# Modulation sums dealt one per weight granule, a vector's end in three steps, and y's parts made from PSUM

## The chip, the core and the metric

The kernel runs on one core of a Trainium2 chip. The metric is the device time of one execution in microseconds (us), lower is better. Of before there are three timed runs and one profiled execution. Engines in the profile: PE is TensorE (matmul), PEld its weight load, DVE is VectorE, ACT ScalarE, POOL GpSimd, SP SyncE, whose queue issues the DMAs.

## The reference

Two layers over 512 latent tokens and 256 context tokens, D = 2048, all fp32. Both begin with a modulated RMS norm whose shift, scale and gate come from a conditioning vector, and end in a gated residual. Cut to what matters here:

```python
def adaln(cond, w, b):
    m = jax.nn.silu(cond) @ w + b          # w is 2048 x 6144, one for each layer
    return jnp.split(m, 3, axis=-1)        # shift, scale, gate

def even_layer(...):
    h = modulate(rms_norm(x, norm_g), sh, sc); hc = the same of ctx
    kc_t, vc_t = split(hc @ w_in[K, V columns])
    au, av, ag, bq, bk, bv, bg = split(h @ w_in)   # each 1024 wide
    q, k = rope(rms_norm per 64 columns of bq, bk)
    o = (softmax(q0 k0) - lam * softmax(q1 k1)) @ v   # 8 heads, 512 x 768
    y = concat(gelu(au) * spatial(gelu(av)) * silu(ag), rms_norm(o) * silu(bg))
    return x + gt * (y @ w_out)

def odd_layer(...):
    h = modulate(rms_norm(x, norm_g), sh, sc)
    a, b, g = split(h @ w_in)              # each 2048 wide
    y = silu(layer_norm(depthwise_conv31(a * sigmoid(b)))) * silu(g)
    return x + gt * (y @ w_out)
```

## The kernel before, in words

**Products in three passes.** Every large product is fp32 made of three matmuls with split operands: high part by high part, high by low, low by high. A weight granule is 1 MB. `load_w` loads it on SP into one of three `raw` buffers (L95), ACT casts it to `whi` (L103), and DVE or POOL subtracts to get `wlo` (L104); `whi` and `wlo` have two buffers each. PE then runs the granule's matmuls (L67).

**The order of the work.** The program is written block after block: the even layer's early modulation (L304), then the blocks K, BV, K (second half), BV, Q (two), AV (two), U (two) of its input product, then the attention, into whose gaps a "fill stream" (`fill_stream`, 18 granules: gates bg and ag, and the first columns of the output product) is dealt, then the output projection (`og` 1 to 3 and a last piece with `x1_last`), then the odd layer: its input product in groups a, b, g with the convolution on DVE (L1106), the layer norm (`ln_chain`), and the last product with `o_w_out`. A scheduler places each instruction in its engine's own queue, by dependencies and priorities; each engine then runs its queue in order. Buffers come from pools that rotate, so a transfer is issued only when the buffer's last reader is done.

**The modulation sums.** Four vectors of 2048 are not needed at once: gt1 (kind 0, the even layer's gate, needed for the output projection), A2 and sh2 (kinds 1 and 2, the odd layer's scale and shift, needed for `x1_last` and `make_h2`) and gt2 (kind 3, needed for the last product). They are made off PE: `ada_jobs` lists 16 steps for each, 64 in all. A step (`ada_step`) loads 1 MB of the modulation weight through the same three `raw` buffers and adds it, scaled by one column of silu(c), to `acc` on DVE (L461 and L463). The sum over the 128 partitions comes at a vector's 16th step: four fp32 matmuls with ones (L468) and a copy on ACT (L472), four matmuls with `sel4` that turn the row into columns (L475) and additions on DVE (L488 to L499), and for three of the kinds a transposition (L482), a copy (L484) and a store to DRAM (L485). Before, all that follows the 16th step at once.

**How they are dealt.** A block calls a hook once for each of its four granules; the hook runs `ada_step` one, two or three times. Before, BV, K, BV take three, two and three, so 32 sums, which are kinds 0 and 1, lie in these blocks; Q and AV take one for each granule (16) and U two (16). All 64 are done by the end of U (the assert ahead of `p12.close()`), and kind 3's end stands there, ahead of the spatial gate's last matmuls (L67, tile z) and the attention.

**Around the attention.** For each of 32 turns PE makes scores S from kk and qq, DVE takes the maximum (mx, L814), ACT the exponential, DVE the weights of the two softmaxes (w, e: L828 to L830), PE transposes (t, L842), ACT and DVE split the transposed values into ph and pl (L112), and at every second turn PE makes oT from ph, pl and vv. Between these stand the fill's matmuls (tile fm).

**The layer norm's chain.** `ln_chain` runs between the granules of the g groups: mean, squares, `rb3`, then for each of 16 tiles `zs` in steps of four, a product with rb3 (L1149), an activation (L1150), a tanh into PSUM (`z4`, L1152) and (th + 1) * z into SBUF (L1153). After the chain comes the product with `sgs` (L1164), and `split` gives y2h (ACT, L111) and y2l (DVE, L112), which are the last product's stationary operands.

Of the kernel before, what the change touches and what calls it, by code (L numbers as in the profile page):

```python
# [19 lines left out]
P = 128  # L20
D = 2048
KT = D // P
# [23 lines left out]
def hybrid_layers_kernel(  # L46
# [403 lines left out]
    ada_state = {"i": 0, "acc": None}  # L450

    def ada_step(zalloc, n=1):
        for _ in range(n):
            if ada_state["i"] >= len(ada_jobs):
                return
            W, c0, kind, jt = ada_jobs[ada_state["i"]]
            ada_state["i"] += 1
            raw = load_raw(W, jt * P, 1, c0, D)[:, 0, :]
            if jt == 0:
                ada_state["acc"] = ap_.tile([P, D], F32, tag="acc", name=nm("acc"))  # L460
                V.tensor_scalar(ada_state["acc"], raw, sc_[:, 0:1], None, op0=ALU.mult)  # L461
            else:
                V.scalar_tensor_tensor(ada_state["acc"], raw, sc_[:, jt : jt + 1], ada_state["acc"], op0=ALU.mult, op1=ALU.add)  # L463
            if jt == KT - 1:
                acc = ada_state["acc"]
                z = zalloc(T)
                for g in range(4):
                    PE.matmul(  # L468
                        z[32 * g : 32 * g + 32, :], ones[:, 0:32], acc[:, g * T : (g + 1) * T],
                        start=True, stop=True, skip_group_check=True,  # L470
                    )
                A.copy(acc[:, 0:T], z)  # L472
                z = zalloc(KT)
                for i in range(4):
                    PE.matmul(z[:, 4 * i : 4 * i + 4], acc[:, i * P : (i + 1) * P], sel4, start=True, stop=True)  # L475
                z = z.rearrange("p (i g) -> p g i", g=4)
                v4 = lambda a: a.rearrange("p (g i) -> p g i", i=4)


                def row_out(col, row_s):  # L480
                    zr = zalloc(P)
                    PE.transpose(zr[:KT, :], col, ident)  # L482
                    rw = cp.tile([KT, P], F32, tag="rw", name=nm("rw"))
                    V.tensor_copy(rw, zr[:KT, :])  # L484
                    SP.dma_start(row_s.rearrange("(k p) -> k p", p=P), rw)  # L485

                if kind == 0:
                    V.tensor_tensor(v4(gt1), z, v4(g1[:, cEB + 2 * KT : cEB + 3 * KT]), op=ALU.add)  # L488
                    row_out(gt1, gt1_s)
                elif kind == 1:  # L490
                    V.tensor_tensor(v4(A2), z, v4(o_b1), op=ALU.add)
                    V.tensor_tensor(A2, A2, g2[:, cOG : cOG + KT], op=ALU.mult)
                    row_out(A2, A2_s)
                elif kind == 2:
                    V.tensor_tensor(v4(sh2), z, v4(g2[:, cOB : cOB + KT]), op=ALU.add)
                else:

                    V.tensor_tensor(v4(gt2), z, v4(g2[:, cOB + 2 * KT : cOB + 3 * KT]), op=ALU.add)
                    V.tensor_scalar(gt2, gt2, 0.25, None, op0=ALU.mult)  # L499
                    row_out(gt2, gt2_s)  # L500


    def qk_post(ps, which, tt, half, tok0, dst, rope):
# [54 lines left out]
        for b in range(NT):  # L558
            qk_post(ps[b], 0, b, half, b * P, q_s, True)

    hook, hook2, hook3 = (lambda gi, n=n: ada_step(zt, n) for n in (1, 2, 3))
    k_done(k0ps, 0)
    ps = m_block(e_w_in, C_BV, both(), psA, "m", hook3)
    v_done(ps, 0)


# [32 lines left out]
        V.tensor_scalar(lam, lam, LAMBDA_INIT, None, op0=ALU.add)  # L599
        V.tensor_scalar(nlam, lam, -1.0, None, op0=ALU.mult)  # L600

    ps = m_block(e_w_in, C_K + 512, both(), psA, "m", hook2)
    k_done(ps, 1)
    ps = m_block(e_w_in, C_BV + 512, both(), psA, "m", hook3)
    v_done(ps, 1)
    for hb in range(2):
        ps = m_block(e_w_in, C_Q + 512 * hb, lat(), psA, "m", hook)
# [43 lines left out]
    for ug in range(2):  # L651
        ps = t_group(e_w_in, C_U + 512 * ug, hm, psA, "m", hook=hook2)
        for j in range(4):
# [14 lines left out]
            mx = bp.tile([P, T], F32, tag="mx", name=nm("mx"))  # L668
            V.tensor_tensor(mx, z, gu, op=ALU.mult)
            SP.dma_start(ug_s[g], mx)  # L670
    assert ada_state["i"] == len(ada_jobs)
    p12.close()


# [38 lines left out]
    def fill_stream():  # L713
        jobs = []
        for i in range(4):
            jobs += [("bg", i, e_w_in, C_BG + 256 * i), ("ag", i, e_w_in, C_AG + 256 * i)]
        jobs.append(("y", 0, e_w_out, 0))
        grans = [(n, gi) for n in range(9) for gi in range(2)]

        def load(n, gi):  # L720
            return load_w(jobs[n][2], gi * 8 * P, 8, jobs[n][3], 2 * P, G)

        nxt = load(0, 0)
        for x, (n, gi) in enumerate(grans):
            kind, i = jobs[n][:2]
            w, nxt = nxt, (load(*grans[x + 1]) if x + 1 < len(grans) else None)
            if gi == 0:
                ps = ps0 if kind == "y" else [None, None]
            if (n, gi) == (7, 1):
                for kt in [0, 1, 2, 3, 4, 5, 8]:  # L730
                    y_load(kt)
            if (n, gi) == (8, 0):
                for kt in range(9, 14):
                    y_load(kt)
            seq = [(j, k) for j in range(2) for k in range(8)]
            if kind == "y" and gi == 1:
                seq = [(j, k) for j in range(2) for k in range(6)] + [(j, k) for k in (6, 7) for j in range(2)]
            for j, k in seq:
                kt = 8 * gi + k
                if ps[j] is None:  # L740
                    ps[j] = psM.tile([P, T], F32, tag="m", name=nm("fm"))
                if kind == "y":
                    if kt == KT - 1 and j == 0:
                        yield "last"
                    yh, yl = ym[kt]
                    wh, wl = w[0][:, k, :], w[1][:, k, :]

                    for i in range(2):
# [12 lines left out]
                if kt == KT - 1:  # L761
                    th = at.tile([P, T], F32, tag="th", bufs=1, name=nm("th"))
                    A.activation(th, ps[j], AF.Tanh, scale=0.5)
                    if kind == "bg":
                        sg = at.tile([P, T], F32, tag="sbg", bufs=2, name=nm("sbg"))
                        V.scalar_tensor_tensor(sg, th, 1.0, ps[j], op0=ALU.add, op1=ALU.mult)
                        sbg[2 * i + j] = sg
                    else:
                        V.scalar_tensor_tensor(th, th, 1.0, ps[j], op0=ALU.add, op1=ALU.mult)
                        y_out(2 * i + j, th, None)  # L770
                yield "more"
# [260 lines left out]
    for og in range(1, 4):  # L1032
        ps = [mt() for _ in range(NT)]
        for gi in range(KT // 4):
            w = load_w(e_w_out, gi * 512, 4, 512 * og, 512)
            m_granule(ps, ystat, *w, range(4 * gi, 4 * gi + 4), 4 * gi)
            if gi == 0 and og == 1:
                for t in range(NT):
                    x1_done(t, 0, 256, ps0[t // 2][:, 256 * (t % 2) : 256 * (t % 2) + 256], 0)
# [5 lines left out]
        for t in range(NT):  # L1045
            x1_done(t, 512 * og, T, ps[t], og)
    load_x(4)
    wl_ = [load_w(e_w_out, gi * 1024, 8, 256, 256) for gi in range(2)]
    ps = [mt() for _ in range(NT)]
    part = lambda t, gi: m_granule([ps[t][:, 0:256]], [ystat[t]], *wl_[gi], range(8 * gi, 8 * gi + 8), 8 * gi)  # L1050
    for t in range(2):
        for gi in range(2):
            part(t, gi)
        x1_last(t, ps[t][:, 0:256])
        if t == 0:
            for u in range(NT):
                scale(u, 3, T)
# [3 lines left out]
    for t in range(2, NT):  # L1061
        part(t, 1)
        x1_last(t, ps[t][:, 0:256])
    make_h2(0, (8, 16))
    a01 = [mt(), mt()]
    first = t_half_steps(o_w_in, 0, h2, a01, G, None, HALVES)
    next(first)
# [64 lines left out]
    def ln_chain():  # L1132
# [14 lines left out]
        rb3 = token_rstd(vacc, 0, T, 1.0 / D)  # L1147
        for i in range(KT):
            V.tensor_tensor(zs[i], zs[i], rb3, op=ALU.mult)  # L1149
            A.activation(zs[i], zs[i], AF.Identity, bias=g2[:, cLB + i : cLB + i + 1], scale=g2[:, cLG + i : cLG + i + 1])  # L1150
            th = z4()
            A.activation(th, zs[i], AF.Tanh, scale=0.5)  # L1152
            V.scalar_tensor_tensor(zs[i], th, 1.0, zs[i], op0=ALU.add, op1=ALU.mult)  # L1153
            if i % 4 == 3:
                yield

    chain = ln_chain()
    for gi in range(1, 4):
        g_group(gi, lambda gi: next(chain, None))
    for _ in chain:  # L1160
        pass
    y2m = []
    for i in range(KT):
        V.tensor_tensor(zs[i], zs[i], sgs[i], op=ALU.mult)  # L1164
        hi, lo = htile("y2h"), htile("y2l")
        split(hi, lo, zs[i])
        y2m.append((hi, lo))


    gt2b = row_tiles(gt2_s, "gt2b")  # L1170
# [56 lines left out]
```

## Time and profile before

| | us |
|---|---|
| median of 3 runs | 1881.65 |
| lowest and highest | 1880.64, 1884.06 |
| the profiled execution | 1877.36 |
| its span | 1875.6 |
| PE busy | 1816.8 |
| DVE busy | 1135.5 |
| ACT busy | 560.2 |
| POOL busy | 452.8 |

The span is the time from the first to the last instruction that the profile shows; 1.8 us of the execution lie outside it. Windows and rows give times from the span's start. A row of the timeline has start, duration, engine, line, operation, tiles (out<-in), the shape, the count, and in brackets the idle time before it with what ended it. PE's matmuls are pipelined, so their durations overlap. The granted clock (PEclk) is 1.00 at full speed.

### The profile page before, as it was taken

To read this page: it belongs to the slowest core of one execution; us is meant where nothing else is said; L and a number is where in the kernel's file an instruction comes from. 1 tells how busy PE (TensorE), PEld (TensorE's weight loads), DVE (VectorE), ACT (ScalarE), POOL (GpSimd) and SP (SyncE) were. 2 spreads that over 40 slices of the span, in tenths; PEclk is the share of its full clock that TensorE was granted. 3 is DMA by queue.
4 is the path that set the end of the run, shared out by engine and by line. 5 is a ranking of instruction groups with operands and counts; after the bars stand their busy time and mean duration, and the time that the engine had idled before them with its cause. 6 is when DMAs were issued, how large, how long until landed. Compare 5 with 4: busy or idle time off the path is not lost.

```text
span 1875.6 us, 21933 instructions
## 1 busy us (share of the span) xinstructions
PE 1816.8 (97%) x8767; PEld 1484.1 (79%) x8767; DVE 1135.5 (61%) x1571; ACT 560.2 (30%) x747; POOL 452.8 (24%) x173
## 2 busy tenths in 40 slices
PE   5998999999999999999999999999999999999998
PEld 2556877788888878888888889888888888887887
DVE  4339528647746626676664345239999999775111
ACT  3322111122233215444442224322222222463110
POOL 0003002001100022232320002234544544444432
PEclk9999999999999989999999999999999999999999
DMA  9998757776756866576555443232233233223441
GB/s 310 334 330 292 233 177 276 262 249 220 243 186 238 308 164 166 151 194 171 167 193 178 147 135 124 68 108 95 90 102 101 90 95 108 90 90 139 138 160 56
DMA packets 208487, 327.34 MB, mean 175 GB/s; under 512 B 10249, under 2 KB 116610, under 8 KB 200194
## 3 DMA queue, kind: packets, MB, share of 16 engines
q1 hardware_dynamic: 208386, 325.94, 53.9%
q8 instruction: 69, 1.13, 0.2%
q14 instruction: 32, 0.26, 0.0%
HBM read 292.33 MB, written 33.58 MB: 174 GB/s over the span
## 4 chain that ended last, share of the span: by engine, by line
PE 85%; DMA 6%; DVE 4%; issue 2%; ACT 1%; POOL 1%; SPq 0%; DVEq 0%; POOLq 0%; ACTq 0%
PE tg L67 30%; PE m L67 18%; PE mb L67 16%; PE fm L67 10%; DMA raw<-in_e_ada_w_dram 2%; PE S L67 2%; DVE acc L463 2%; PE oT L67 2%; DMA raw<-in_o_ada_w_dram 2%; PE z L304 2%; PE t L842 1%; DVE wlo L104 1%; PE z L67 1%; DMA x<-in_x_dram 1%; PE fm L752 1%
## 5 line engine op out<-in xcount | busy, mean ns | idle before, releaser
L104 POOL TENSOR_TENSOR wlo<-raw,whi 128x2048 fp32r<-128x2048 f32 x80 | 370.0, 4624 | 647.0 <-ACT whi L103 639.6
L103 ACT CAST whi<-raw 128x2048 fp32r<-128x2048 f32 x136 | 259.8, 1910 | 740.2 <-PE tg L67 214.1
L1106 DVE SCALAR_TENSOR_TENSOR z<-y,dwc,z 128x512 f32<-128x512 f32 x480 | 319.2, 744 | 0.1
L67 PE MATMUL tg<-h2h,wlo 128*128 128x512 f32 x704 | 274.7, 390 | 0.0
L67 PE MATMUL tg<-h2l,whi 128*128 128x512 f32 x704 | 273.9, 389 | 0.0
L67 PE MATMUL tg<-h2h,whi 128*128 128x512 f32 x704 | 270.4, 389 | 0.0
L104 DVE TENSOR_TENSOR wlo<-raw,whi 128x2048 fp32r<-128x2048 f32 x56 | 128.1, 2288 | 146.3 <-ACT whi L103 146.3
L67 PE MATMUL mb<-whi,hhi 128*128 128x512 f32 x512 | 204.8, 403 | 5.3 <-DVE tn L512 3.4
L67 PE MATMUL mb<-wlo,hhi 128*128 128x512 f32 x512 | 203.4, 397 | 2.3 <-DVE wlo L104 2.3
L67 PE MATMUL mb<-whi,hlo 128*128 128x512 f32 x512 | 203.6, 398 | 0.0
L463 DVE SCALAR_TENSOR_TENSOR acc<-raw,silu_c,acc 128x2048 f32<-128x2048 f32 x60 | 140.9, 2349 | 87.2 <-DMA raw<-in_o_ada_w_dram 65.1
L67 PEld LDWEIGHTS tg<-h2h,wlo 128*128 128x128 f32 x704 | 132.1, 188 | 28.0 <-issue 0.5
L67 PEld LDWEIGHTS tg<-h2l,whi 128*128 128x128 f32 x704 | 132.1, 188 | 27.8 <-issue 0.5
L67 PEld LDWEIGHTS tg<-h2h,whi 128*128 128x128 f32 x704 | 132.1, 188 | 27.4
L194 POOL TENSOR_TENSOR rs<-ms,mhalf 128x8 f32<-128x8 f32 x20 | 44.6, 2244 | 394.4 <-DVE ms L193 394.4
L67 PEld LDWEIGHTS mb<-whi,hhi 128*128 128x128 f32 x512 | 98.1, 192 | 39.7 <-issue 14.0
L67 PEld LDWEIGHTS mb<-wlo,hhi 128*128 128x128 f32 x512 | 98.3, 192 | 23.0 <-DVE wlo L104 3.1
L67 PEld LDWEIGHTS mb<-whi,hlo 128*128 128x128 f32 x512 | 98.3, 192 | 20.9
L67 PE MATMUL fm<-hhi,whi 128*128 128x512 f32 x256 | 106.7, 417 | 0.0
L67 PE MATMUL m<-wlo,y2h 128*128 128x512 f32 x256 | 99.8, 390 | 2.6 <-POOL wlo L104 2.6
L67 PE MATMUL fm<-hlo,whi 128*128 128x512 f32 x256 | 101.1, 395 | 0.0
L67 PE MATMUL fm<-hhi,wlo 128*128 128x512 f32 x256 | 100.8, 394 | 0.0
(259 smaller groups left out, 3024.9 us busy)
## 6 DMA issues: line engine op xcount, KB each, us to landing
raw<-in_e_w_in_dram SPq DMA_DIRECT2D x56, 1024.0 KB, 5.2
raw<-in_o_ada_w_dram SPq DMA_DIRECT2D x48, 1024.0 KB, 5.8
raw<-in_o_w_in_dram SPq DMA_DIRECT2D x48, 1024.0 KB, 5.1
raw<-in_e_ada_w_dram SPq DMA_DIRECT2D x64, 512.0 KB, 7.5
raw<-in_e_ada_w_dram SPq DMA_DIRECT2D x16, 1024.0 KB, 5.6
raw<-in_e_w_out_dram SPq DMA_DIRECT2D x16, 1024.0 KB, 5.9
raw<-in_o_w_out_dram SPq DMA_DIRECT2D x16, 1024.0 KB, 5.9
qq<-q_s SPq DMA_DIRECT2D x16, 512.0 KB, 8.7
```

What stands on the lines that cost most here:

```text
L67: return PE.matmul(o, l, r, start=start, stop=stop)
L103: A.copy(hi, raw)
L104: (lo_eng or V).tensor_tensor(lo, raw, hi.bitcast(F32), op=ALU.subtract)
L194: G.tensor_tensor(dst, tmp, mhalf[:, 0:1].broadcast_to([P, n]), op=ALU.pow)
L304: PE.matmul(ada_ps[j][32 * g : 32 * g + 32, 0 : 2 * nc_], S[:, kt, :], raw[:, i, :], start=(kt < 4), stop=(kt >= KT - 4), skip_group_check ...
L463: V.scalar_tensor_tensor(ada_state["acc"], raw, sc_[:, jt : jt + 1], ada_state["acc"], op0=ALU.mult, op1=ALU.add)
L752: PE.matmul(o_, a[:, ts_], b, start=(kt == 0 and i == 0 and a is yh and b is wh), stop=(kt == KT - 1 and i == 1 and a is yl), skip_group_c ...
L842: PE.transpose(z[:, k * P : (k + 1) * P], e[:, (k0 + k) * P : (k0 + k + 1) * P], ident)
L1106: V.scalar_tensor_tensor(zi if t == TAPS - 1 else z, y2[:, t : t + T], w(t), z, op0=ALU.mult, op1=ALU.add)
```

## The change

**The sums.** `hook3` is gone and BV, K, BV take one step for each granule (12). Q and AV keep one and U two, so 44 steps lie ahead of the attention instead of 64. In the fill stream three granules of four take one, and the output projection takes one for each of its 12 granules; the assert moves behind it. **A vector's end.** The 16th step only puts three functions, `spread`, `columns` and `row`, into `ada_tail`; each later call runs one of them, and `spread` alone takes the place of a sum. Kind 3's last steps stand behind `x1_last`. **y's parts.** The products with rb3 are all made first. Where the gate `sgs[i]` is there already, (th + 1) * z and the product with it are written to th in PSUM, and `y2_split` makes the parts from there; the others are made after the chain, through a PSUM tile too.

```diff
     def ada_step(zalloc, n=1):
+        if ada_tail:
+            f = ada_tail.pop(0)
+            f(zalloc)
+            if f.__name__ == "spread":
+                return
         for _ in range(n):
...
             if jt == KT - 1:
-                acc = ada_state["acc"]
-                z = zalloc(T)
...
+                ada_tail.extend(ada_finish(kind, ada_state["acc"]))
+                return
...
+    def ada_finish(kind, acc):
+        col, b_, row_s = bias[kind]()
+
+        def spread(zalloc):
+            z = zalloc(T)
+            for g in range(4):
+                PE.matmul(
+                    z[32 * g : 32 * g + 32, :], ones[:, 0:32], acc[:, g * T : (g + 1) * T],
+                    start=True, stop=True, skip_group_check=True,
+                )
+            A.copy(acc[:, 0:T], z)
+
+        def columns(zalloc):
+            z = zalloc(KT)
+            for i in range(4):
+                PE.matmul(z[:, 4 * i : 4 * i + 4], acc[:, i * P : (i + 1) * P], sel4, start=True, stop=True)
...
+        def row(zalloc):
+            zr = zalloc(P)
+            PE.transpose(zr[:KT, :], col, ident)
...
+            SP.dma_start(row_s.rearrange("(k p) -> k p", p=P), rw)
+
+        return [spread, columns] + ([row] if row_s is not None else [])
...
-    ps = m_block(e_w_in, C_BV, both(), psA, "m", hook3)
+    ps = m_block(e_w_in, C_BV, both(), psA, "m", hook)
...
-    ps = m_block(e_w_in, C_K + 512, both(), psA, "m", hook2)
+    ps = m_block(e_w_in, C_K + 512, both(), psA, "m", hook)
...
-    ps = m_block(e_w_in, C_BV + 512, both(), psA, "m", hook3)
+    ps = m_block(e_w_in, C_BV + 512, both(), psA, "m", hook)
...
-    assert ada_state["i"] == len(ada_jobs)
     p12.close()
...
             if gi == 0:
                 ps = ps0 if kind == "y" else [None, None]
+            if x % 4 != 3:
+                ada_step(zt3, 1)
...
             m_granule(ps, ystat, *w, range(4 * gi, 4 * gi + 4), 4 * gi)
+            ada_step(z4, 1)
...
+    assert ada_state["i"] == len(ada_jobs)
...
         x1_last(t, ps[t][:, 0:256])
+        ada_step(z4)
...
+    while ada_tail:
+        ada_step(z4)
...
         for i in range(KT):
             V.tensor_tensor(zs[i], zs[i], rb3, op=ALU.mult)
+        for i in range(KT):
             A.activation(zs[i], zs[i], AF.Identity, bias=g2[:, cLB + i : cLB + i + 1], scale=g2[:, cLG + i : cLG + i + 1])
             th = z4()
             A.activation(th, zs[i], AF.Tanh, scale=0.5)
-            V.scalar_tensor_tensor(zs[i], th, 1.0, zs[i], op0=ALU.add, op1=ALU.mult)
+            if sgs[i] is None:
+                V.scalar_tensor_tensor(zs[i], th, 1.0, zs[i], op0=ALU.add, op1=ALU.mult)
+            else:
+                V.scalar_tensor_tensor(th, th, 1.0, zs[i], op0=ALU.add, op1=ALU.mult)
+                V.tensor_tensor(th, th, sgs[i], op=ALU.mult)
+                y2_split(i, th)
             if i % 4 == 3:
                 yield
+                if i == 7:
+                    yield
...
-    y2m = []
     for i in range(KT):
-        V.tensor_tensor(zs[i], zs[i], sgs[i], op=ALU.mult)
-        hi, lo = htile("y2h"), htile("y2l")
-        split(hi, lo, zs[i])
-        y2m.append((hi, lo))
+        if y2m[i] is None:
+            z = z4()
+            V.tensor_tensor(z, zs[i], sgs[i], op=ALU.mult)
+            y2_split(i, z)
```

On DVE, at the end of the first K block, whose results tn, rot and ms are k's normalisation and rotation while the BV block's matmuls begin, there stood before:

```order
L463 SCALAR_TENSOR_TENSOR acc_1524<-raw_1610,silu_c,acc_1524 128x2048
L512 TENSOR_TENSOR tn_1301<-mb_330,rs_1297 128x512
L193 TENSOR_SCALAR ms_1346<-ms_1346 128x8
L193 TENSOR_SCALAR ms_1371<-ms_1371 128x8
L508 TENSOR_REDUCE ms_1396<-sq_1394 128x8
L512 TENSOR_TENSOR tn_1326<-mb_331,rs_1322 128x512
L463 SCALAR_TENSOR_TENSOR acc_1524<-raw_1613,silu_c,acc_1524 128x2048
L104 TENSOR_TENSOR wlo_1535<-raw_1532,whi_1534 128x2048
L520 TENSOR_TENSOR rot_1303<-tn_1301,SG_1291 128x16x16 x2
```

Now the same tiles come so:

```order
L522 TENSOR_TENSOR tn_1301<-mb_330,rs_1297 128x512
L193 TENSOR_SCALAR ms_1371<-ms_1371 128x8
L468 SCALAR_TENSOR_TENSOR acc_1524<-raw_1685,silu_c,acc_1524 128x2048
L530 TENSOR_TENSOR rot_1303<-tn_1301,SG_1291 128x16x16 x2
L522 TENSOR_TENSOR tn_1326<-mb_331,rs_1322 128x512
L518 TENSOR_REDUCE ms_1396<-sq_1394 128x8
L104 TENSOR_TENSOR wlo_1529<-raw_1526,whi_1528 128x2048
```

One sum stands among these posts where there were two, and the posts follow each other more closely behind it. On PE, at the end of U (tiles tg) and ahead of the spatial gate (z_4594 and on), there stood before:

```order
L67 MATMUL tg_4333<-hlo_1185,whi_4516 128x512
L468 MATMUL z_4574<-acc_4069,ones 32x512 x4
L475 MATMUL z_4580<-sel_84,acc_4069 128x4 x4
L482 MATMUL z_4587<-ident,gt_98 16x128
L67 MATMUL z_4594<-wsh,vnh_3981 128x128
L67 MATMUL z_4594<-wsl,vnh_3981 128x128
```

Now U's last matmuls are followed by the gate's second tile and the fill's first (fm):

```order
L67 MATMUL tg_4235<-hlo_1185,whi_4431 128x512
L67 MATMUL z_4510<-wsl,vnh_3908 128x128
L67 MATMUL z_4510<-wsh,vnl_3912 128x128
L67 MATMUL z_4529<-wsh,vnh_3887 128x128
...
L67 MATMUL z_4548<-wsh,vnl_3912 128x128
L67 MATMUL fm_4605<-hhi_390,whi_4592 128x512
```

The end of kind 3 is gone from this place, and the gate's first tile and most of its second stand earlier, among U's own matmuls. On DVE in the attention, at the end of the sixth turn, there stood before, between the next turn's maximum (mx) and its weights (w):

```order
L814 TENSOR_REDUCE mx_5253<-S_5244 128x1 x2
L112 TENSOR_TENSOR pl_5191<-t_859_5263,ph_5190 128x4x128
L112 TENSOR_TENSOR pl_5191<-t_860_5270,ph_5190 128x2x128
L828 RECIPROCAL w_864_5280<-s_861_5275 128x1
L829 TENSOR_SCALAR w_864_5280<-w_864_5280,s_821_5065,nlam 128x1
```

Now:

```order
L825 TENSOR_REDUCE mx_5162<-S_5153 128x1 x2
L468 SCALAR_TENSOR_TENSOR acc_4299<-raw_5423,silu_c,acc_4299 128x2048
L112 TENSOR_TENSOR pl_5100<-t_832_5172,ph_5099 128x4x128
L112 TENSOR_TENSOR pl_5100<-t_833_5179,ph_5099 128x2x128
L839 RECIPROCAL w_837_5189<-s_834_5184 128x1
```

A sum has come between the maximum and pl, which this turn's value product on PE reads. Such a place, with the sum ahead of pl, is there at seven of the attention's odd turns.

More of the change, by code (lines that the diff above doesn't have):

```diff
@@ L464, in ada_step @@
             if jt == KT - 1:
-                acc = ada_state["acc"]
-                z = zalloc(T)
[L467 to L500, printed above, removed]
@@ new lines, in ada_step @@
+                ada_tail.extend(ada_finish(kind, ada_state["acc"]))
+                return
+    ada_tail = []
+    bias = {0: lambda: (gt1, g1[:, cEB + 2 * KT : cEB + 3 * KT], gt1_s), 1: lambda: (A2, o_b1, A2_s),
+            2: lambda: (sh2, g2[:, cOB : cOB + KT], None), 3: lambda: (gt2, g2[:, cOB + 2 * KT : cOB + 3 * KT], gt2_s)}
+    def ada_finish(kind, acc):
[12 more added lines that the diff above has]
+                PE.matmul(z[:, 4 * i : 4 * i + 4], acc[:, i * P : (i + 1) * P], sel4, start=True, stop=True)
+            v4 = lambda a: a.rearrange("p (g i) -> p g i", i=4)
+            V.tensor_tensor(v4(col), z.rearrange("p (i g) -> p g i", g=4), v4(b_), op=ALU.add)
+            if kind == 1:
+                V.tensor_tensor(col, col, g2[:, cOG : cOG + KT], op=ALU.mult)
+            if kind == 3:
+                V.tensor_scalar(col, col, 0.25, None, op0=ALU.mult)
+        def row(zalloc):
+            zr = zalloc(P)
+            PE.transpose(zr[:KT, :], col, ident)
+            rw = cp.tile([KT, P], F32, tag="rw", name=nm("rw"))
+            V.tensor_copy(rw, zr[:KT, :])
+            SP.dma_start(row_s.rearrange("(k p) -> k p", p=P), rw)
+        return [spread, columns] + ([row] if row_s is not None else [])
@@ L559, in q_done @@
             qk_post(ps[b], 0, b, half, b * P, q_s, True)
-    hook, hook2, hook3 = (lambda gi, n=n: ada_step(zt, n) for n in (1, 2, 3))
+    hook, hook2 = (lambda gi, n=n: ada_step(zt, n) for n in (1, 2))
     k_done(k0ps, 0)
-    ps = m_block(e_w_in, C_BV, both(), psA, "m", hook3)
+    ps = m_block(e_w_in, C_BV, both(), psA, "m", hook)
     v_done(ps, 0)
@@ L1152, in ln_chain, with y2_split @@
             A.activation(th, zs[i], AF.Tanh, scale=0.5)
-            V.scalar_tensor_tensor(zs[i], th, 1.0, zs[i], op0=ALU.add, op1=ALU.mult)
+            if sgs[i] is None:
[4 more added lines that the diff above has]
+                y2_split(i, th)
             if i % 4 == 3:
                 yield
+                if i == 7:
+                    yield
+    y2m = [None] * KT
+    def y2_split(i, z):
+        hi, lo = htile("y2h"), htile("y2l")
+        split(hi, lo, z)
+        y2m[i] = (hi, lo)
     chain = ln_chain()
```

## The prediction

> **What bounds the kernel now.** The page's first part is read first: it says that TensorE (PE) is the bound.
>
> ```profile
> PE 1816.8 (97%) x8767; PEld 1484.1 (79%) x8767; DVE 1135.5 (61%) x1571; ACT 560.2 (30%) x747; POOL 452.8 (24%) x173
> ```
>
> PE's instructions hardly change, so the time can only come from where PE stands still or runs at a lower clock. The windows view shows where that is. Its columns are busy time and count of PE, PEld, DVE, ACT and POOL, then PE's mean granted clock, the DMA share and GB/s.
>
> ```profile
> 150.00:200.00 50.00, 42.77 (x185) 33.97 (x184) 44.00 (x61) 10.12 (x15) 16.85 (x6) 0.93 0.76 254
> 200.00:250.00 50.00, 46.27 (x205) 37.88 (x203) 26.65 (x22) 10.65 (x12) 0.00 (x0) 0.98 0.86 285
> 250.00:300.00 50.00, 49.73 (x217) 39.77 (x217) 16.12 (x12) 6.21 (x4) 0.00 (x0) 0.95 0.47 163
> 300.00:350.00 50.00, 46.70 (x202) 37.34 (x202) 45.81 (x52) 7.75 (x11) 13.46 (x6) 0.97 0.80 273
> 350.00:400.00 50.00, 49.59 (x229) 39.90 (x228) 21.89 (x18) 12.51 (x13) 0.00 (x0) 1.00 0.77 236
> 400.00:650.00 250.00, 249.81 (x1153) 206.51 (x1152) 160.34 (x141) 70.49 (x74) 16.43 (x12) 1.00 0.69 240
> 650.00:700.00 50.00, 45.36 (x205) 38.31 (x204) 11.86 (x13) 8.60 (x8) 12.49 (x3) 0.83 0.64 186
> 700.00:950.00 250.00, 250.00 (x1350) 211.66 (x1350) 163.85 (x275) 119.64 (x213) 71.69 (x21) 1.00 0.63 175
> 1000.00:1150.00 150.00, 150.00 (x741) 127.56 (x740) 63.23 (x76) 39.19 (x55) 1.10 (x2) 1.00 0.49 160
> 1650.00:1725.00 75.00, 72.35 (x317) 58.85 (x316) 56.51 (x70) 43.59 (x59) 32.77 (x7) 1.00 0.32 112
> ```
>
> Four places matter. From 150 to 400 (BV, K and BV blocks) PE is idle for 14.9 us (50 less its busy time, five rows) and loses 8.5 us to the clock (50 times what the clock lacks of 1.00): 23.4 us, in the rows where DVE is busiest. At 650 to 700 it loses 4.6 idle and 8.5 to the clock. At 1650 to 1725 it is idle for 2.7. The attention, 700 to 950, is full: nothing can be gained there and everything can be lost. The waits view names the releasers (total us, times, longest):
>
> ```profile
> PE z L580 <- DMA dwr<-in_o_dw_w_dram: 4.0, 2, 3.7
> PE mb L67 <- DVE tn L512: 3.6, 4, 2.1
> PE z L482 <- DVE gt L499: 3.2, 1, 3.2
> PE m L67 <- POOL wlo L104: 2.6, 2, 1.9
> PE z L531 <- DVE rot L526: 2.4, 1, 2.4
> PE mb L67 <- DVE wlo L104: 2.3, 2, 1.9
> PE z L475 <- ACT acc L472: 1.5, 1, 1.5
> ```
>
> **Part A: fewer sums in 150 to 400.** DVE's groups from 143 to 400 hold the sums.
>
> ```profile
> L463 DVE SCALAR_TENSOR_TENSOR acc<-raw,silu_c,acc 128x2048 f32<-128x2048 f32 x31 | 72.8, 2348 | 35.6 <-DMA raw<-in_e_ada_w_dram 21.6 <-DMA raw<-in_o_ada_w_dram 13.8
> ```
>
> Of the 32 sums that these three blocks are dealt, 12 stay. That removes 20 x 2.35 = 47 us of DVE and 20 MB of loads, and most of the 35.6 us in which DVE stood in order behind a sum whose granule had not landed, with k's normalisation (tn, rot) and the weights' wlo queued behind it. What PE waits for there is just that: tn, rot, wlo, and dwr, whose transposes stand behind the same queue. What stays are the posts' own chains at three block ends, with a POOL power in each. I take that a quarter of the 23.4 remains (about 6) and that the gain is -17. Matmuls are shown with their pipelined tails, so gaps under 0.4 us do not show as idle and the true loss is some us above 23.4; hence the bounds -23 and, if two thirds of the waits belong to the posts themselves, -9.
>
> **Part B: the end of U and the start of the attention.** PE's rows here, then two windows of 5 us (PE busy, its clock, the DMA share, GB/s):
>
> ```profile
> 664.70 1.06 PE L468 MATMUL z<-acc,ones 128*32 128x512 f32 x8
> 667.25 1.05 PE L475 MATMUL z<-sel,acc 128*128 128x4 f32 x8 [1.48 <-ACT acc L472]
> 671.46 0.37 PE L482 MATMUL z<-ident,gt 128*16 128x128 f32 x1 [3.16 <-DVE gt L499]
> ...
> 681.77 0.73 PE L67 MATMUL fm<-hhi,whi 128*128 128x512 f32 x1
> ...
> 685.29 0.40 PE L67 MATMUL fm<-hlo,whi 128*128 128x512 f32 x1
> ```
> ```profile
> 670.00:675.00 5.00, 3.54 (x18) 0.50 0.24 69
> 680.00:685.00 5.00, 5.00 (x18) 0.50 0.28 103
> ```
>
> The last vector's end holds PE from 664.70 to 671.46, and the 48 spatial-gate matmuls behind it run at half clock: 681.77 - 671.46 = 10.3 us, where the full clock needs 5.1. The fill's first matmuls run at half clock until 685.29, which loses half of 3.5 us. So 6.8 + 5.1 + 1.7 = 13.6 us go if no vector ends here. The end's own PE time (1.06 + 1.05 + 0.37 = 2.5) is moved, not saved: gain -11. The bounds are -13.6 and -4: three sums of kind 2 now stand on DVE among the gate's steps, and the first kk and qq loads stand on SP behind the granule of the third of them. If they go out 7 us later than the fill can cover, PE stands for 7 at the first S.
>
> A rule bears on this row. The Trainium skill, "TensorE: Matmul & The Clock Gate", Part 1: The HAM clock gate, has PE back at full rate after one busy window of about 3.4 us. By that rule the clock would have been back by about 675 and the gain would be some 5 us less. The trace disagrees: PE was busy from 671.46 and stayed at 0.50 until 685, so the measured 13.6 stands.
>
> **Part C: 13 sums in the attention.** First DVE's rows around two turns of the attention, then PE's, then what a load takes there (KB, median us to landing) and one load's issue on SP.
>
> ```profile
> 753.00 1.82 DVE L814 TENSOR_REDUCE mx<-S 128x1 f32<-128x768 f32 x2
> 754.73 1.01 DVE L112 TENSOR_TENSOR pl<-t,ph 128x512 fp32r<-128x512 f32 x2
> ...
> 806.16 1.82 DVE L814 TENSOR_REDUCE mx<-S 128x1 f32<-128x768 f32 x2
> ...
> 808.61 0.69 DVE L112 TENSOR_TENSOR pl<-t,ph 128x512 fp32r<-128x512 f32 x1
> ```
> ```profile
> 755.47 0.39 PE L67 MATMUL oT<-pl,vv 128*128 128x256 f32 x1
> ...
> 810.21 0.28 PE L67 MATMUL oT<-pl,vv 128*128 128x256 f32 x1
> ```
> ```profile
> raw<-in_e_w_in_dram SPq DMA_DIRECT2D x11, 1024.0 KB, 5.2
> qq<-q_s SPq DMA_DIRECT2D x12, 512.0 KB, 8.7
> ```
> ```profile
> 803.85 0.39 SPq L95 DMA_DIRECT2D raw<-in_e_w_in_dram  x1
> ```
>
> The value product oT takes pl almost as it is made: pl ends at 809.30, oT starts at 810.21, a slack of 0.9; at 755.47 there is none. In the changed order the sum stands between mx and pl at seven such turns, and it costs 2.35 there. At the second place PE would stand for 2.35 - 0.9 = 1.4, at the first for 2.3. If the sum's granule is issued when GpSimd's wlo frees a buffer (a granule issues at 803.85) it lands at about 809.1, the sum ends at 811.4 and pl at 812.1: PE stands for 1.9. Seven times 1.4 to 2.3 is 10 to 16; the other six stand where DVE has time. I take +11. The bounds: +3 if the granules come early and only the turns without slack pay (one or two of 2.3), and +22 if nine stand for 2.4. DVE has room in total (163.85 of 250, plus 31), so it is the place that costs, not the sum of work.
>
> **Part D: y's parts from PSUM.** One DVE, one POOL and one ACT row of the tail.
>
> ```profile
> 1702.86 4.62 DVE L1164 TENSOR_TENSOR z<-z,sg 128x512 f32<-128x512 f32 x1
> ```
> ```profile
> 1702.36 4.56 POOL L104 TENSOR_TENSOR wlo<-raw,whi 128x2048 fp32r<-128x2048 f32 x1 [10.79 <-ACT whi L103]
> ```
> ```profile
> 1711.64 1.91 ACT L103 CAST whi<-raw 128x2048 fp32r<-128x2048 f32 x1
> ```
>
> A product of two SBUF tiles that starts beside GpSimd's wlo ends only with it (4.62 here); the weights' whi then comes late on ACT, wlo later, and PE waits 2.6 us in two pieces (the waits view). With th in PSUM the product has one SBUF input. Gain -2.6, bounds 0 and -3: the same number of products runs, and each now holds one of few PSUM buffers.
>
> **Part E: 12 sums in the output projection and the last end.** There DVE is busy for 63 of 150 us and DMA at 0.49, so 11 x 2.35 hide: 0. The last vector's end in three steps, its PE time, and buffers of x1's stage: +1 to +2, taken as +1; bound +5.
>
> **The sum.** -17 - 11 + 11 - 2.6 + 1 = -18.6 on the profiled execution's 1877.4 us (span 1875.6 and 1.8 around it): 1858.8. That execution lies 4.3 under the median of 1881.65, so against the runs the forecast is 1881.65 - 18.6 = 1863.
>
> **The rivals.** (1) Slower: late granules in the attention. A sum's load stands on SP among kk, qq and vv, and qq takes 8.7 where a weight takes 5.2. If the granules land like qq, each of the sums ahead of a pl costs 1.9 + 3.5 = 5.4, and seven cost 38 instead of 11: 1863 + 27 = 1890. It turns slower than before, by over 3.8 us, once the attention gives back over 29.6 + 3.8 us (the gains of A, B, D less E, and what can be told), which is 4.8 per sum. For it: the empty slack at 755.47 and no idle PE to absorb anything. Against: DMA at 0.63 there. Chance 0.12.
>
> (2) The shared port. This row and the wlo beside it:
>
> ```profile
> 743.55 4.59 POOL L104 TENSOR_TENSOR wlo<-raw,whi 128x2048 fp32r<-128x2048 f32 x1 [12.72 <-ACT whi L103]
> ```
> ```profile
> 745.98 2.71 DVE L698 TENSOR_TENSOR th<-th,ugl 128x512 f32<-128x512 f32 x1
> ```
>
> A product, 0.69 at that size elsewhere (pl at 808.61), took 2.71 because it started inside wlo. A sum reads two SBUF tiles too. If ten of the 13 fall into a wlo and wait 2 us more, the time is 1863 + 20 = 1883: no change. Against it: the sum's buffer often comes free only when wlo ends, so it runs between two of them. Chance 0.07. The Trainium skill, "SBUF — State Buffer", SBUF: two separate sides, states this as an exclusive lock held for a whole instruction; the row agrees.
>
> (3) The block ends are the posts' own. If A gives only -9 and the kk loads of B come late (B -4), the sum is -4.6: 1877, still faster by a little. Chance 0.14.
>
> **How the numbers follow.** The forecast has 0.67. A measurement of this kernel can tell about 0.2%, 3.8 us, from no change. Faster: the forecast and four fifths of (3), with its better side: 0.67 + 0.11 = 0.78; the same: the rest of (3) and most of (2), 0.08; slower: (1) and the rest of (2), 0.14. The range: the better ends of A to E together (-23 - 13.6 + 3 - 3 + 0) give 1845, and short of that 1848; on the upper side it reaches through (3) and (2) to 1885, leaving out (1).
>
> **What would show it.** In the profile after: PE's row 150 to 400 with some 6 us idle and lost; no end at the gate, the clock at 1.00 there; in the attention, waits of oT for pl of 1.4 to 2.3 us at seven turns, and acc rows on DVE just ahead; no product over 1 us beside wlo in the tail. It is wrong if the attention shows no oT waits (then some 11 us faster), if the block ends keep their waits, or if kk and qq hold S at the first turn.

## The result and the profile after

The changed kernel takes 1894.15 us (median of 4 runs, 1892.11 to 1895.61) against 1881.14 for the kernel before (4 runs, 1877.98 to 1884.06). The ratio is 1.0069, with a 95% interval from 1.0049 to 1.0088: it is slower by 0.7%, where the forecast was 1863 and its range ended at 1885. The profiled execution took 1892.11, its span is 1890.3.

First the page's busy times after. They say that PE's work is the same, so the difference lies again in waits and in the clock.

```profile
PE 1819.3 (96%) x8767; PEld 1486.8 (79%) x8767; DVE 1125.1 (60%) x1571; ACT 560.2 (30%) x747; POOL 446.7 (24%) x173
```

The windows view after, with PE's busy time and count, its granted clock, the DMA share and GB/s:

```profile
150.00:200.00 50.00, 49.21 (x230) 1.00 0.58 185
200.00:250.00 50.00, 49.59 (x221) 1.00 0.70 214
250.00:300.00 50.00, 50.00 (x226) 1.00 0.40 132
300.00:350.00 50.00, 50.00 (x230) 1.00 0.61 186
350.00:400.00 50.00, 50.00 (x222) 1.00 0.61 186
400.00:650.00 250.00, 244.52 (x1149) 0.99 0.63 217
650.00:700.00 50.00, 42.59 (x188) 0.91 0.85 232
700.00:950.00 250.00, 230.17 (x1191) 0.95 0.62 180
1000.00:1150.00 150.00, 146.69 (x695) 1.00 0.67 226
1650.00:1725.00 75.00, 75.00 (x334) 1.00 0.38 127
```

From 150 to 400 PE is idle for 1.2 us where it was 14.9, at full clock throughout. In the tail it is full. But the attention, full before, has lost 19.8 us to idle time and 5% of its clock, and 400 to 650 lost 5.5. The waits view of PE says for what:

```profile
PE oT L67 <- DVE pl L112: 17.9, 9, 5.5
...
PE S L67 <- issue: 6.0, 1, 6.0
PE t L879 <- DVE pl L112: 5.2, 3, 3.5
PE m L67 <- DVE wlo L104: 4.1, 4, 1.7
PE z L635 <- DMA wsr<-in_e_a_ws_dram: 4.0, 1, 4.0
```

The first three lines stand in the attention; the third is where kind 2's end stands (its matmuls at 852.2 and 893.0, the longest waits of t at 859.02 and 901.66). To place the loss exactly, the times of the same matmuls are set side by side, from the span's start. The table is worked out from the first and last start of each tile in the two traces.

| PE reaches | before | after | difference |
|---|---|---|---|
| the end of the second BV block | 388.2 | 360.4 | -27.8 |
| the end of AV | 569.3 | 546.9 | -22.4 |
| the end of U | 664.4 | 644.9 | -19.4 |
| the fill's first matmul | 681.8 | 650.2 | -31.6 |
| the fill's last matmul | 1006.1 | 1020.9 | +14.7 |
| the end of the output projection | 1155.4 | 1174.9 | +19.5 |
| the last product's first matmul | 1693.2 | 1711.2 | +18.0 |
| the last matmul | 1870.3 | 1885.0 | +14.8 |

The changed kernel was 31.6 us ahead when the attention began and 14.7 behind when it ended. From the fill's first matmul to its last, the attention takes 370.7 us instead of 324.3: 46.4 more. This is the tile view of fm in the kernel before, then after (least, median and longest ns, first and last start):

```profile
L67 PE MATMUL fm<-hhi,whi x256: 387/396/792, 681.8 to 959.6; 128*128 128x512 f32 x128
...
L752 PE MATMUL fm<-whi,yl x64: 277/283/386, 961.9 to 1006.1; 128*128 128x256 f32 x64
```
```profile
L67 PE MATMUL fm<-hhi,whi x256: 387/397/1117, 650.2 to 974.1; 128*128 128x512 f32 x128
...
L763 PE MATMUL fm<-whi,yl x64: 277/283/288, 976.4 to 1020.9; 128*128 128x256 f32 x64
```

One turn shows how such a stall is made. These are rows of after: SP's issue of the sum's granule, DVE's three steps, and PE's value product.

```profile
734.69 0.42 SPq L95 DMA_DIRECT2D raw<-in_o_ada_w_dram  x1
```
```profile
737.95 1.82 DVE L825 TENSOR_REDUCE mx<-S 128x1 f32<-128x768 f32 x2
743.08 2.35 DVE L468 SCALAR_TENSOR_TENSOR acc<-raw,silu_c,acc 128x2048 f32<-128x2048 f32 x1 [3.31 <-DMA raw<-in_o_ada_w_dram]
745.35 1.01 DVE L112 TENSOR_TENSOR pl<-t,ph 128x512 fp32r<-128x512 f32 x2
```
```profile
746.09 0.58 PE L67 MATMUL oT<-pl,vv 128*128 128x256 f32 x1 [5.50 <-DVE pl L112]
```

The granule was asked for at 734.69 and had landed at 743.08, 8.4 us later. DVE stood for 3.3 us in front of the sum with pl behind it, then took 2.35 for the sum, and PE stood for both: 5.5.

### The profile page after: what moved, and what is told of

Its sections match the earlier page's. It is cut to its first block, busy times and chain, and to the rows that moved or that the text cites. A ratio compares the mean times of both kernels' runs of the same rounds, so it can differ in the third digit from the quotient of the medians.

```text
span 1890.3 us, 21892 instructions
## 1 busy us (share of the span) xinstructions
PE 1819.3 (96%) x8767; PEld 1486.8 (79%) x8767; DVE 1125.1 (60%) x1571; ACT 560.2 (30%) x747; POOL 446.7 (24%) x173
## 4 chain that ended last, share of the span: by engine, by line
PE 75%; DMA 10%; DVE 6%; issue 4%; ACT 2%; POOL 1%; SPq 1%; DVEq 0%; ACTq 0%; POOLq 0%
PE tg L67 28%; PE mb L67 19%; PE m L67 14%; PE fm L67 5%; DMA raw<-in_o_ada_w_dram 4%; DVE acc L468 2%; PE oT L67 2%; DVE wlo L104 2%; PE z L304 2%; PE S L67 2%; ACT whi L103 1%; DMA raw<-in_e_w_in_dram 1%; POOL wlo L104 1%; DMA q_s<-qklo 1%; DMA raw<-in_e_ada_w_dram 1%
## 5 line engine op out<-in xcount | busy, mean ns | idle before, releaser
L468 DVE SCALAR_TENSOR_TENSOR acc<-raw,silu_c,acc 128x2048 f32<-128x2048 f32 x60 | 145.2, 2420 | 132.6 <-DMA raw<-in_o_ada_w_dram 85.0
L67 PEld LDWEIGHTS tg<-h2h,wlo 128*128 128x128 f32 x704 | 132.2, 188 | 27.9 <-issue 0.5
L67 PEld LDWEIGHTS tg<-h2l,whi 128*128 128x128 f32 x704 | 132.2, 188 | 27.9 <-issue 0.5
L194 POOL TENSOR_TENSOR rs<-ms,mhalf 128x8 f32<-128x8 f32 x20 | 38.2, 1923 | 375.1 <-DVE ms L193 375.1
L67 PEld LDWEIGHTS mb<-whi,hhi 128*128 128x128 f32 x512 | 97.1, 190 | 32.1 <-issue 11.7
L67 PEld LDWEIGHTS mb<-wlo,hhi 128*128 128x128 f32 x512 | 97.0, 190 | 19.4 <-DVE wlo L104 0.2
```

The source lines that it names most:

```text
L67: return PE.matmul(o, l, r, start=start, stop=stop)
L194: G.tensor_tensor(dst, tmp, mhalf[:, 0:1].broadcast_to([P, n]), op=ALU.pow)
```

## The experiments

Theory 1: the loss lies in the attention, and is that of the sums' places on DVE together with the wait for their granules. Rivals: a sum costs PE about the same in any block; or the extra 13 MB of loads are to blame. Lines of the trace differ by a few from kernel to kernel.

**No sum in the fill.**

```diff
-    ps = m_block(e_w_in, C_Q + 512 * hb, lat(), psA, "m", hook)
+    ps = m_block(e_w_in, C_Q + 512 * hb, lat(), psA, "m", hook2)
...
-    ps = m_block(e_w_in, C_AV + 512 * hb, lat(), psA, "m", hook)
+    ps = m_block(e_w_in, C_AV + 512 * hb, lat(), psA, "m", hook2)
...
-            if x % 4 != 3:
-                ada_step(zt3, 1)
```

> The changed kernel with no sum in the attention's fill; Q and AV take two for each granule instead, the rest goes to the output projection. Theory 1 (what the change lost is lost in the attention, where each sum stands in DVE's order ahead of pl): the attention is back at its length of before, the fill's first to last matmul 278 us instead of 324, and the time is 1894 - 46 = 1848, up to 1855 if Q and AV give some back. Theory 2 (a sum costs PE about the same wherever it stands): the loss moves to Q and AV and the time is over 1875.

Measured: 1856.88 us, ratio to before 0.9875 (0.9861 to 0.9890). The fill takes 325.3 us, as before (324.3), and the waits of oT are down to 2.3. (The 278 and 324 of the expectation end at the last fm<-hhi; counted so, this run has 278.4.)

```profile
PE oT L67 <- DVE pl L112: 2.3, 3, 1.4
```

So the whole loss belongs to the sums, their loads and the end that were dealt to the attention. The time is 2 us above the expected span, because Q, AV and U give back 18 us of the 25.7 gained by the end of BV (after gives back 8). The first rival is right in so far as sums there are not free: some 16 more, with kind 2's end among them, cost 10 us more, 0.6 each, against 46 us for 13 and the same end in the attention.

**Loads without sums.** The fill's sums are left out, except the first of kind 3, and the loads stay. A granule that nothing reads also gives its buffer back sooner.

```diff
-            else:
+            elif not fill:
                 V.scalar_tensor_tensor(ada_state["acc"], raw, ...)
...
-                ada_step(zt3, 1)
+                ada_step(zt3, 1, True)
```

> The changed kernel whose sums in the fill are left out, all but the first of kind 3, while their granules are still loaded; so sh2 and gt2 lack these terms. Theory 1 (the sum's place on DVE, with the wait for its granule): the waits of oT and of t for pl go, about 23 us and what half clock follows them, and the time is about 1860. Theory 2 (the loads themselves, 13 MB in SP's queue and on the DMA rings, hold up kk, qq and the weights): the time stays at 1885 or more.

Measured: 1865.45 us, ratio 0.9922 (0.9906 to 0.9939). The fill takes 343.5 us, 27 less than after and 19 more than before. In the attention's waits, oT's have gone, and S's and t's have stayed:

```profile
PE S L67 <- issue: 5.8, 1, 5.8
PE t L879 <- DVE pl L112: 4.9, 2, 3.5
PE oT L67 <- DVE pl L112: 1.0, 2, 0.6
```

So the sums on DVE are 27 of the 46, and 19 is something else that this kernel still has: the loads, kind 2's end, and kind 3's first sum.

**The sum reads a weight granule.** The sums of the fill stand where they stood, but read the granule that the fill loads anyway; the vectors are sums of other numbers.

```diff
-            raw = load_raw(W, jt * P, 1, c0, D)[:, 0, :]
+            raw = last_raw[0].rearrange("p k n -> p (k n)") if fill else load_raw(W, jt * P, 1, c0, D)[:, 0, :]
```

> The changed kernel whose sums in the fill read the weight granule that has been loaded there anyway instead of a granule of their own; so no extra load runs in the attention, the sums stand between mx and pl at the same kind of turn, and sh2 and gt2 are sums of other numbers. If the place on DVE alone costs what was forecast (1.4 to 2.3 at about nine turns), the attention gives back 11 to 18 instead of 46: 1860 to 1868. If the landing of the granule is all of it, about 1850; if the place is all of it, about 1890.

Measured: 1894.71 us, ratio 1.0082 (1.0066 to 1.0097): no better than the changed kernel, and 366.8 us for the fill. So a loss of this size comes without the 13 MB of extra loads: they are not what costs in the middle of the attention. It does not part place from landing, as was meant, since DVE still waits in front of these sums, now for the weight granule. The loads do matter in one place: without them the first S waits no more, as these rows of DVE's and of PE's waits show.

```profile
DVE acc L471 <- DMA raw<-in_e_w_in_dram: 12.2, 3, 4.6
```
```profile
PE S L67 <- issue: 0.4, 1, 0.4
```

**Behind the weights.** The fill's loads stay where they are; a sum from the fourth granule on is queued on DVE behind a turn's e, a turn or more after its load.

```diff
+            if fill:
+                late.append([0, add])
+                return
...
-        V.scalar_tensor_tensor(e[0], e[1], w1[:, 0:1], e[0], op0=ALU.mult, op1=ALU.add)
+        last = V.scalar_tensor_tensor(e[0], e[1], w1[:, 0:1], e[0], op0=ALU.mult, op1=ALU.add)
+        if late and late[0][0] > 1:
+            with tc.issue_after(last.ins):
+                late.pop(0)[1]()
```

> The changed kernel with the same loads, but each sum of the fill from its fourth granule on is queued on DVE behind a turn's weights (e), a turn or more after its granule was asked for, so it stands ahead of no pl and its granule has landed. Theory (each sum's place ahead of pl, with the wait for its granule): the waits of oT for pl are under 3 us in sum, the wait of S at the start stays, and the time is 1854 to 1864. Rival (13 MB of extra loads and held buffers are what costs): 1880 or more.

**Landed, at the same place.** As the last, but the sum stands between mx and pl of an odd turn.

```diff
+            if qt % 2 and late and late[0][0] > 1:
+                with tc.issue_after(last.ins):
+                    s = late.pop(0)[1]()
+            turn(h, qt, s)
...
+            with tc.issue_after(s.ins) if s else ExitStack():
                 split(ph[...], pl[...], ...)
```

> As the run before, but each of these sums stands between mx and pl of an odd turn, as in the changed kernel, with its granule landed a turn before. It shows what the place alone costs. By the forecast's price (2.35 less a slack of 0 to 0.9) ten such turns cost 14 to 23 more than the run behind the weights: 1870 to 1885. If the wait for the granule is all of it, both runs are alike; if the place is all of it, this one is at 1890 or more.

Measured: 1873.09 us behind the weights, ratio 0.9976 (0.9965 to 0.9987), and 1881.68 at the old place, ratio 1.0024 (1.0009 to 1.0039). The first is above its expected span, the second within it; but they differ by 8.6, where 14 to 23 was expected. The waits of oT are, behind the weights and at the old place:

```profile
PE oT L67 <- DVE pl L112: 0.6, 1, 0.6
```
```profile
PE oT L67 <- DVE pl L112: 10.0, 9, 2.8
```

The fill takes 352.2 and 361.1 us. The 9 us between them are not the price of the place, since the first kernel loses 7 us behind the last turn's scores, which neither the second nor the changed kernel does. This table tells how much later than in the kernel before a turn's first S starts, counted in each kernel from the fill's first matmul (in us, worked out from the starts of S and fm in the traces, with turns numbered from 0; differences of 0.1 from the fill times above are rounding):

| S of turn | changed kernel | loads without sums | behind the weights | landed, at the old place |
|---|---|---|---|---|
| 1 | 8.5 | 7.1 | 9.6 | 9.8 |
| 17 | 31.5 | 7.1 | 9.6 | 19.7 |
| 22 | 43.2 | 18.8 | 20.8 | 30.8 |
| 31 | 46.1 | 18.9 | 21.0 | 36.7 |
| the fill's last matmul | 46.3 | 19.2 | 27.9 | 36.7 |

The changed kernel's loss has three parts. The start costs 8.5 us. Between turns 17 and 22 kind 2's end stands, no sum is ahead of an odd turn's pl, and all four kernels lose 11 to 12. The sums cost the other 26 (23.0 up to turn 17, 2.9 behind turn 22). At the old place, with their granules landed, the sums cost 15.8 (9.9 and 5.9), 1.8 for each of the nine that stand ahead of a pl, where the forecast had 1.4 to 2.3; behind the weights they cost nothing. In the changed kernel three sums (at 717.5, 743.1 and 805.5) keep DVE waiting for their granules for 3.0 to 3.4 us, and set the next S back by 6.1 to 8.1 each, 20.6 together; two that have landed (782.8 and 947.6) set it back by 0.7 and 0.8. So the late granules, with the half clock behind each stall, are most of the 26. How the 26 divide exactly stays open, since the sums stand at other turns in the two kernels.

What the kernel behind the weights still loses is seen in its windows (PE busy, clock, DMA share, GB/s):

```profile
650.00:700.00 50.00, 43.26 (x194) 0.87 0.83 224
700.00:800.00 100.00, 100.00 (x543) 1.00 0.70 201
800.00:900.00 100.00, 95.60 (x498) 0.95 0.61 178
900.00:950.00 50.00, 50.00 (x274) 1.00 0.81 247
950.00:1000.00 50.00, 43.41 (x303) 0.93 0.64 220
```

From 700 to 800 and from 900 to 950 sums run and PE loses nothing. The losses lie at the start, at 800 to 900, where kind 2 ends, and at the end of the attention, where sums of the output projection are already queued and one stands ahead of the last turn's e. This last loss is this kernel's own.

**The start.** No sums at the fill's first three granules, more in the output projection; the others as in the changed kernel.

```diff
-            if x % 4 != 3:
+            if x > 2 and x % 4 != 3:
...
-            ada_step(z4, 1)
+            ada_step(z4, 2 if og == 1 else 1)
```

> The changed kernel without the sums of the fill's first three granules, which are made up for in the output projection; the others stand ahead of pl as in the changed kernel. If kk and qq were late for the first S because they stood on SP behind the third of these granules, S starts 17 us after the fill's first matmul, as without sums in the fill, not 23.6, and the half clock behind it goes: 8 to 10 us of the attention. If the first S waits for something else, it stays at 23.6.

Measured: 1904.58 us, ratio 1.0126 (1.0100 to 1.0151), and the first S now starts 17.9 us after the fill's first matmul: all but 1.3 us of the wait of S is gone, and at turn 1 this kernel is level with the kernel before. But the whole is slower, since eight of kind 2's sums now stand ahead of a pl at odd turns, where five did:

```profile
PE oT L67 <- DVE pl L112: 29.8, 10, 5.8
...
PE S L67 <- ACT th L774: 1.3, 1, 1.3
```

In the changed kernel the third sum's granule is asked for at 655.01, ahead of the gate's last store (ug_s, 655.61), and has landed at 661.85; only then are kk and qq issued, and S starts 10 us later. What kk's issue waits for, by SP's waits, is the landing of that store, for 6.4 us. Where the sums read weight granules, the store was issued at 658.54 and kk already at 660.83. That it is the load and not the sum follows from the two runs above: with loads and no sums S waits 5.8, with sums and no loads 0.4. These are DVE's, SP's and PE's rows of the changed kernel:

```profile
661.85 2.35 DVE L468 SCALAR_TENSOR_TENSOR acc<-raw,silu_c,acc 128x2048 f32<-128x2048 f32 x1 [6.27 <-DMA raw<-in_o_ada_w_dram]
```
```profile
655.01 0.33 SPq L95 DMA_DIRECT2D raw<-in_o_ada_w_dram  x1
655.61 0.33 SPq L680 DMA_DIRECT2D ug_s<-mx  x1
662.58 1.32 SPq L801 DMA_DIRECT2D kk<-k_s  x2
663.95 1.26 SPq L804 DMA_DIRECT2D qq<-q_s  x2
```
```profile
673.83 2.90 PE L67 MATMUL S<-kk,qq 128*128 128x256 f32 x8 [6.02 <-issue]
```

**The end at once.** The kernel without sums in the fill, with each vector's end made at its 16th sum, as before the change.

```diff
-                ada_tail.extend(ada_finish(kind, ada_state["acc"]))
-                return
+                for f in ada_finish(kind, ada_state["acc"]):
+                    f(zalloc)
```

> The run without sums in the fill, with each vector's end made at once at its sixteenth sum as in the kernel before. Theory (the end costs PE its chain of waits, 1.5 and 3.2 us and a spell of half clock, at each of four places): 8 to 16 us more than with the end in three steps, 1865 to 1873. Rival (only the place ahead of the gate was bad, and the three steps bring nothing of their own): no difference, 1857.

Measured: 1854.72 us, ratio 0.9878 (0.9860 to 0.9896), beside 1856.88 and 0.9875 with the end in three steps. The intervals overlap: the rival holds, the three steps bring nothing that can be measured of their own here. The gain of part B came from where kind 3 ends: with the end at once, the end of U and the fill's first matmul are 6.7 us apart, and 17.4 in the kernel before.

**The tail alone.** The kernel before with y's parts from PSUM and nothing else.

> The kernel before with the third part of the change alone, y's parts from PSUM. Theory: PE's two waits for wlo in the last product go, 3 us: 1878 against 1881. Rival (the gain of the tail in the changed kernel comes of something else that the change moved): no difference.

Measured: 1876.20 us against 1879.68 beside it, ratio 0.9981 (0.9972 to 0.9990). The last matmul starts 3.1 us earlier, and no wait of PE is left after 1650, as in the changed kernel.

**Eight sums in the middle.** One sum for each of granules 3 to 10, behind the weights; none at the start or the end; no vector ends in the attention; the output projection takes two for each granule.

```diff
-            if x % 4 != 3:
-                ada_step(zt3, 1)
+            if 3 <= x <= 10:
+                ada_step(zt3, 1, True)
...
-            ada_step(z4, 1)
+            ada_step(z4, 2)
```

> The changed kernel with no sum at the fill's first three granules, one behind a turn's weights for each of granules 3 to 10, none after, and two for each granule of the output projection. If the middle of the attention holds eight sums for nothing as long as they stand behind the weights and no vector ends there, the fill's first to last matmul takes 324 to 327 us as before; the blocks keep their gain (-28 at the end of BV, -19 at the end of U), and the time is about 1852 plus what the output projection gives back, 3 to 10: 1855 to 1862. If sums cost in the attention wherever they stand, it is 335 or more there and the time over 1865.

Measured: 1851.21 us (1849.60 to 1852.16), ratio 0.9841 (0.9824 to 0.9858): the fastest kernel of this study. It is faster than both kernels, by 30 and by 43 us, and under its expected span by 4. The fill takes 324.8 us with eight sums in it. Its windows:

```profile
650.00:700.00 50.00, 48.56 (x240) 1.00 0.76 192
700.00:800.00 100.00, 99.71 (x546) 1.00 0.75 226
800.00:900.00 100.00, 100.00 (x544) 1.00 0.69 195
```

**The same with two on Q and one in the output projection.**

```diff
-    ps = m_block(e_w_in, C_Q + 512 * hb, lat(), psA, "m", hook)
+    ps = m_block(e_w_in, C_Q + 512 * hb, lat(), psA, "m", hook2)
...
-            ada_step(z4, 2)
+            ada_step(z4, 1)
```

> As the run before, but Q takes two for each granule and the output projection one. Q with two loses 4 to 8 more than with one, the output projection 5 at the most, kind 2 ends in U. The attention as before, 324 to 327. Time 1850 to 1858.

Measured: 1862.21 us, ratio 0.9898 (0.9878 to 0.9917): a miss, 4 us above the span. The fill takes 332.7 us, 8 more than in the run before. Kind 2's sixteenth sum now comes in U, so that its end falls to the fill's first calls, and PE's longest wait in the attention is a t behind it. Q and AV lose another 7.4. A further 3.8 is there already when the early modulation ends, ahead of every sum, and the output projection gives 5.4 back.

```profile
PE t L894 <- DVE pl L112: 3.0, 1, 3.0
```

## Why the prediction was wrong

**The step that failed is part C**, "13 sums in the attention", taken as +11 with +22 as its upper bound; it measured +46.4. The mechanism was seen: the sum ahead of pl, the turn without slack, PE waiting for both. The place itself was priced about right (1.8 for each of nine landed sums). Two other things were mis-sized or not counted, and a third was weighed rightly.

- The landing. The forecast took 5.2 us for a granule, from the weights' row before, so about 1 us of waiting. In the attention after it is longer (KB, median us to landing):

```profile
raw<-in_o_ada_w_dram SPq DMA_DIRECT2D x15, 1024.0 KB, 6.7
raw<-in_e_w_in_dram SPq DMA_DIRECT2D x14, 1024.0 KB, 7.8
```

  At the turn shown above it was 8.4. This is rival (1), which had put 8.7 and 1890; it had a chance of 0.12. DVE waited 3.0 to 3.4 at three sums ahead of a pl, and these three cost 20.6 with the half clock behind them. The sums together cost 26, not 11.

- What was charged elsewhere or not at all. The first S late by 6 us, with a spell of half clock behind it, was named as a bound of part B ("PE stands for 7 at the first S") and left out of the value; the start cost 8.5. For kind 2's end, which now falls into the attention, the sum has no term, and no reason is given; it cost 11.7 between turns 17 and 22. The run with such an end at the fill's start, and its sums behind the weights, gave back 8.

- The shared port, rival (2). The tile view of the sums after has least, median and longest ns:

```profile
L468 DVE SCALAR_TENSOR_TENSOR acc<-raw,silu_c,acc x60: 2330/2351/5605, 148.7 to 1109.3; 128x2048 f32<-128x2048 f32 x60
L466 DVE TENSOR_SCALAR acc<-raw,silu_c x4: 1277/1280/4493, 143.9 to 895.0; 128x2048 f32<-128x2048 f32 x4
```

  The two longest stand beside a wlo of GpSimd and end after it:

```profile
895.01 4.49 DVE L466 TENSOR_SCALAR acc<-raw,silu_c 128x2048 f32<-128x2048 f32 x1
959.10 5.61 DVE L468 SCALAR_TENSOR_TENSOR acc<-raw,silu_c,acc 128x2048 f32<-128x2048 f32 x1
```
```profile
893.81 4.60 POOL L104 TENSOR_TENSOR wlo<-raw,whi 128x2048 fp32r<-128x2048 f32 x1 [12.72 <-ACT whi L103]
957.95 4.61 POOL L104 TENSOR_TENSOR wlo<-raw,whi 128x2048 fp32r<-128x2048 f32 x1 [13.15 <-ACT whi L103]
```

  It was as the forecast had it, a mechanism at two or three of the 13 sums, not at ten. The Trainium skill, "SBUF — State Buffer", SBUF: two separate sides, has the port as an exclusive lock for a whole instruction; these rows agree, the first with a tensor-scalar that has only one SBUF input, a case that the Trainium skill's same section puts down to the 2-port mode; no run here shows the mode.

**Part A** was right in kind and too small: -17 forecast, -27.8 measured (-24.3 to -28.7 in the experiments that deal these blocks alike). Of the 27.8, 2.5 are there already at the last matmul of the early modulation (139.9 before, 137.5 after), ahead of the first sum. From there to the end of the second BV block the gain is 25.3, and 25.3 to 25.9 in the experiments, beyond the bound of -23. The row-wise sum of idle time and clock, 23.4, was a floor, as the text had said, and all of it went; the posts' own chains cost PE about 1 us, not 6.

**Part B**: -11 forecast. From the end of U to the fill's first matmul the gain is 12.2. About 2.4 of it is only moved: 22 of the 48 gate matmuls, at 0.11 us each, now stand ahead of U's end. Of the half clock a spell is left, 0.75 in the window 650 to 655.

**Part D**: -2.6 forecast, -3.2 measured from the last product's first matmul to its last, in the changed kernel and alone.

**Part E**: +1 forecast, +4.8 measured in the output projection (its bound was +5), 1.9 of it in waits for wlo where there were none, and 1.5 regained behind it. Not foreseen was that Q, AV and U, whose sums per granule did not change, give back 8.4. A 4.0 us wait for wsr, a load queued among the sums', is the largest piece that the waits view names, and the 2.4 of moved gate matmuls are another.

The sum of the measured parts is -27.8 + 8.4 - 12.2 + 46.4 + 4.8 - 1.5 - 3.2 = +14.9, the difference of the last matmul (14.8). The median differs by 13.0.

The chances were wrong where the text's own evidence spoke: a stage in which PE is full, with turns that have no slack, was given an upper bound from one mechanism, although the forecast knew three (landing, port, SP's queue) that add up there. That a slower kernel needed 4.8 for each of seven sums was taken as remote; the sums came to 3.7 for each of seven, and the start and kind 2's end to 20 more. Rival (3) was also added up wrong: with E's +1 its sum is -3.6, not -4.6, which is inside the 3.8 that the text could not tell from no change.

What stays open: how the 26 us of the sums divide between place and landing; what makes up the rest of part E, and of the 8.4 in Q, AV and U. Of kind 2's end only the place and the loss are known, not which of its steps costs how much.

## What to carry to other kernels

Work that is moved into a stage where the bound engine never waits has to be placed, not only dealt: behind the step with slack, with its data asked for a turn earlier, it costs nothing (eight sums in 324.8 us). Ahead of the step that the bound engine waits for, it costs part of its duration when its data has landed (1.8 of 2.35 us on average), and 6 to 8 us where the data comes 3 us late. A load that joins an in-order queue must be checked against what is queued behind it, and a change whose parts gain in one stage and lose in another is best split at once by the times at which the same matmul is reached.

## What was not expected of the hardware

The shared port holds a tensor-scalar with a single SBUF input too: 1.28 us alone and 4.49 beside GpSimd's subtraction (893.81 to 898.41). And PE's clock can fall to half at short stalls inside a stage of full work, which makes a stall dearer than its length. With the 5.5 us of the turn shown above the window's clock was 0.73; in the changed kernel a stall of 1.42 at 859.02 is followed by 0.83 from 860 to 870, while one of 1.39 at 698.33 left it at 1.00.

```profile
740.00:750.00 10.00, 4.50 (x22) 0.73 0.48 168
```
